# The second attention stream of the first half starts after the first one's end

## Chip, cores and metric

One core of a Trainium2 chip runs the whole program. The metric is the device time of one execution in microseconds, the median of several runs. TensorE is called PE, VectorE DVE, ScalarE ACT, GpSimd POOL and SyncE SP, as in the profile.

## What is computed

Two layers on 1024 tokens of width 1024, in fp32. Layer 0 mixes tokens by a recurrent scan (RWKV-7, eight heads) and a sliding-window attention (eight query heads, two key/value heads, window 128, with sinks) side by side; layer 1 by a convolution. Each layer then has an MLP with squared ReLU.

```python
def hybrid_mixer(h, w_in, ...):
    p = h @ w_in
    y_rwkv = rwkv7_time_mix(p[..., :o1], ...)
    y_att = sliding_window_sink_attention(q, k, v, sinks)
    return jnp.concatenate([y_rwkv, y_att], axis=-1) @ w_out

for layer in range(2):
    h = rmsnorm(x, norm_mix_g[layer])
    x = x + (hybrid_mixer(h, ...) if layer == 0 else conformer_conv(h, ...))
    x = x + sqrelu_mlp(rmsnorm(x, norm_ffn_g[layer]), w1, w2)
return rmsnorm(x, final_norm_g)
```

Attention takes, per block of 128 queries, the 256 keys of this and the last block, adds a slope by distance, takes the maximum with the sink, and divides the exponentials by their sum and the sink's.

## The kernel before

The tokens are worked in two halves of 512. Every large matrix product goes by `mm3` (L302 to L310): weights and inputs are split into a high part in fp32r and the rest, and three products of 128x512 are summed (L308, L309, L310). The weights come through SP's queue (L286), ACT rounds the high part (L291), and DVE or POOL takes the rest (`lo`, L272).

The first 800 us or so are woven. `weave` (L82) runs a base, the weight products of the two halves, the output projection of half 0 and its MLP, and beside it other generators: "A" and "B" run the scans (`scans`, L1100; B takes head pairs 0 and 2 of half 0, A takes 1 and 3 of half 0 and then all four of half 1), "n" the norm ahead of the MLP of half 0 (`norm0`, L505), and "0" and "1" the two streams of attention (`att`, L1024). A generator yields either a number, a time on the weave's own clock before which it isn't taken up again, or a flag that another sets. That clock is a planner's, advanced by written-down costs of PE work; the table LAG holds the pauses. Of the generators that are due the first in the order "1BAn0p" goes, as long as their share of PE work stays in bounds. The order so made is PE's order for good; the orders of the other engines and of the DMA queues are made by the scheduler of the language.

One stream of attention has two head pairs (stream 0 pairs 0 and 1, stream 1 pairs 2 and 3). For a pair it reads the queries back from DRAM into "raw" on SP's queue (`queries`, L1012; one buffer for both streams), rounds them on ACT (L1019) and takes the rest on DVE (L272), and makes two passes of 256 tokens (`attention`, L868): scores on PE (L890, L892) into PSUM tiles "at", of which there are two for both streams; slope and mask on DVE (L895), the maximum (L899), exponentials on ACT (L905), the division (L913 on ACT, L914 on DVE), transposes on PE (L923), copies on ACT (L924), the product with the values on PE (L932) and a copy on DVE (L936). The pause ATT stands between scores and transposes.

A scan of one head pair inverts 16x16 blocks on DVE (L705, L707), sends them through DRAM and back (L714 waits for that DMA), and joins them by four steps of block products on PE (L730), each with copies ahead of the next: L736 on ACT ahead of the second, L739 and L741 on DVE ahead of the third, L746 on ACT and L747 on DVE ahead of the fourth. The norm of half 0 sums squares on DVE (L455, L457, L477), transposes the sums on PE (L479), spreads the root by a product (L490, copied by ACT in L492), and scales on DVE (L517), with the split on ACT (L518) and DVE (L272). The residual sums of the output projection are L1192.

In half 0 stream 1 waits for the flag "0kv", set as soon as keys and values are in; in half 1 for "1z0", set when stream 0 has ended:

```python
        else:
            yield "1z0" if hf else "0kv"
```

Of the kernel before, what the change touches and what calls it, by code (L numbers as in the profile page):

```python
# [45 lines left out]
class Net:  # L46
# [977 lines left out]
    def att(self, hf, z):  # L1024

        if z == 0:
            for j in (18, 19):
                yield f"{hf}k{j}"
            if hf == 1:
                yield "mi1"  # L1030
                yield "att0"
            yield LAG["load"]
            yield from self.att_in(hf)
            self.done.add(f"{hf}kv")
        else:
            yield "1z0" if hf else "0kv"
        for i in (2 * z, 2 * z + 1):
            yield f"{hf}k{14 + i}"
            qs = self.queries(hf, i, z)
            yield LAG["query"]  # L1040
            yield from self.attention(hf, i, z, qs, self.mi[hf][4 + i])
        self.done.add(f"{hf}z{z}")
        self.natt += 1
        if self.natt == 2 * hf + 2:
            self.done.add(f"att{hf}")
# [400 lines left out]
    def run(self):  # L1446
# [75 lines left out]
        with self.tc.manual_schedule(engines={mybir.EngineType.PE}):  # L1522
            gs = {"p": params, "A": lambda: self.scans(0, [(0, 1), (0, 3), (1, 0), (1, 1), (1, 2), (1, 3)]), "B": scans_b,
                  "n": self.norm0, "0": lambda: att(0), "1": lambda: att(1)}
            self.weave(main(), *[gs[c]() for c in ORDER])
# [78 lines left out]
```

## Time and profile before

| | |
|---|---|
| median of 3 runs | 2353.58 us (2350.31 to 2355.61) |
| the profiled execution | 2348.04 us |
| its span, first to last instruction | 2346.3 us |
| PE busy | 2296.8 us (98%) |
| DVE busy | 1568.4 us (67%) |
| ACT busy | 1036.3 us (44%) |
| POOL busy | 349.1 us (15%) |
| mean granted clock of PE | 0.995 |

The span is the profiler's, from the first to the last instruction; the execution's own time has the launch around it. PE's idle time is the span less its busy time. A wait is read in the timeline, in square brackets behind the instruction that waited: how long its engine was idle, and what ended that.

### The profile page before, as it was taken

The page shows a single profiled execution, that of the slowest core. Times are in us where ns is not written, and L with a number is a line of the kernel's source. Part 1 is how long each engine was busy: PE and PEld are TensorE (multiplying, and loading weights), DVE is VectorE, ACT ScalarE, POOL GpSimd, SP SyncE. Part 2 cuts the span into 40 slices and gives each one's busy share as a digit, 9 for nine tenths or more (in the row PEclk, how much of TensorE's full clock was granted, in tenths as well). Part 3 has the DMA queues.
Part 4 walks back from the last instruction along what each step waited for, and adds up shares of the span by engine and source line. Part 5 has one row for each costly group of instructions (what it writes and reads, how often), then busy time and mean ns, then how long its engine had stood idle before and what let it go on. Part 6 is the DMA issues. An engine that isn't in the chain of part 4 may idle for free.

```text
span 2346.3 us, 38479 instructions
## 1 busy us (share of the span) xinstructions
PE 2296.8 (98%) x14535; PEld 1848.9 (79%) x14535; DVE 1568.4 (67%) x2707; ACT 1036.3 (44%) x1855; POOL 349.1 (15%) x333
## 2 busy tenths in 40 slices
PE   8989999999999999999999999999999999999998
PEld 6767777777777777878888888888878878888887
DVE  7876855767575655389876554789999746433334
ACT  6545625455353433353433464524433634433333
POOL 0001000000000000121000000215555422221221
PEclk9999999999999999999999999999999999999999
DMA  7445334445444454447666664563323333333332
GB/s 215 128 113 144 99 92 133 122 145 155 136 135 154 153 160 138 150 153 215 196 190 197 191 187 148 163 174 95 99 87 97 95 99 103 120 96 99 95 99 85
DMA packets 417933, 320.11 MB, mean 136 GB/s; under 512 B 44642, under 2 KB 360276, under 8 KB 417748
## 3 DMA queue, kind: packets, MB, share of 16 engines
q1 hardware_dynamic: 413684, 309.79, 44.0%
q0 software_dynamic: 2176, 4.19, 0.7%
q10 hardware_dynamic: 1888, 3.67, 0.5%
q8 instruction: 114, 1.87, 0.3%
q14 instruction: 71, 0.58, 0.1%
HBM read 257.29 MB, written 60.29 MB: 135 GB/s over the span
## 4 chain that ended last, share of the span: by engine, by line
PE 78%; DVE 15%; ACT 3%; issue 2%; DMA 2%; POOL 0%; SPq 0%; DVEq 0%; ACTq 0%; POOLq 0%
PE mm L308 23%; PE mm L309 22%; PE mm L310 22%; DVE acc L1318 8%; DVE hidl L272 1%; PE sc L648 1%; DVE x L1250 1%; PE sc L730 1%; PE sc L813 1%; PE at L932 1%; PE sc L767 1%; DVE wlo L272 1%; PE at L923 1%; PE sc L673 0%; DVE h L272 0%
## 5 line engine op out<-in xcount | busy, mean ns | idle before, releaser
L291 ACT CAST whi<-wraw 128x512 fp32r<-128x512 f32 x720 | 445.8, 620 | 979.6 <-PE mm L309 894.6
L308 PE MATMUL mm<-h,whi 128*128 128x512 f32 x1792 | 722.0, 404 | 7.4 <-DVE x L1250 3.0
L310 PE MATMUL mm<-h,wlo 128*128 128x512 f32 x1792 | 701.4, 392 | 1.0 <-POOL wlo L272 1.0
L309 PE MATMUL mm<-h,whi 128*128 128x512 f32 x1792 | 700.2, 391 | 1.3 <-DVE h L272 1.0
L1318 DVE SCALAR_TENSOR_TENSOR acc<-u,par,acc 128x512 f32<-128x512 f32 x480 | 429.3, 904 | 10.0
L272 DVE TENSOR_TENSOR wlo<-wraw,whi 128x512 fp32r<-128x512 f32 x370 | 260.7, 706 | 233.5 <-ACT whi L291 218.4
L308 PEld LDWEIGHTS mm<-h,whi 128*128 128x128 f32 x1792 | 337.2, 188 | 89.1 <-issue 12.5
L310 PEld LDWEIGHTS mm<-h,wlo 128*128 128x128 f32 x1792 | 337.4, 188 | 74.8 <-POOL wlo L272 1.9
L309 PEld LDWEIGHTS mm<-h,whi 128*128 128x128 f32 x1792 | 337.8, 188 | 68.7 <-issue 2.4
L308 PE MATMUL mm<-hidh,whi 128*128 128x512 f32 x992 | 389.7, 396 | 0.1
L309 PE MATMUL mm<-hidl,whi 128*128 128x512 f32 x992 | 386.2, 390 | 1.1 <-DVE hidl L272 0.9
L310 PE MATMUL mm<-hidh,wlo 128*128 128x512 f32 x992 | 384.5, 390 | 0.9 <-POOL wlo L272 0.9
L272 POOL TENSOR_TENSOR wlo<-wraw,whi 128x512 fp32r<-128x512 f32 x190 | 270.9, 1427 | 648.9 <-ACT whi L291 632.5
L1250 DVE TENSOR_TENSOR x<-mm,x 128x512 f32<-128x512 f32 x248 | 166.7, 687 | 85.0 <-PE mm L310 84.7
L308 PEld LDWEIGHTS mm<-hidh,whi 128*128 128x128 f32 x992 | 186.2, 188 | 43.0 <-issue 3.2
L309 PEld LDWEIGHTS mm<-hidl,whi 128*128 128x128 f32 x992 | 186.3, 188 | 40.7 <-DVE hidl L272 2.4
L310 PEld LDWEIGHTS mm<-hidh,wlo 128*128 128x128 f32 x992 | 186.2, 188 | 40.4 <-POOL wlo L272 1.3
L272 DVE TENSOR_TENSOR hidl<-rel,hidh 128x512 fp32r<-128x512 f32 x117 | 89.2, 763 | 78.1 <-ACT hidh L1227 76.7
L1223 ACT ACTIVATE rel<-rel 128x512 f32<-128x512 f32 x128 | 80.6, 633 | 4.6 <-DVE hidl L272 1.2
L1229 DVE CAST hidh<-rel 128x512 fp32r<-128x512 f32 x68 | 32.8, 485 | 71.2 <-ACT rel L1223 70.9
L1222 ACT ACTIVATE rel<-mm 128x512 f32<-128x512 f32 x128 | 75.6, 592 | 2.2 <-DVE hidl L272 2.0
L518 ACT CAST h<-nt 128x512 fp32r<-128x512 f32 x48 | 29.4, 622 | 34.7 <-DVE nt L517 34.3
(374 smaller groups left out, 2072.4 us busy)
## 6 DMA issues: line engine op xcount, KB each, us to landing
wraw<-in_mlp_w_dram SPq DMA_DIRECT2D x512, 256.0 KB
lo<-wlo SPq DMA_DIRECT2D x160, 256.0 KB
wlo<-lo SPq DMA_DIRECT2D x160, 256.0 KB
wraw<-in_cv_pw_w_dram SPq DMA_DIRECT2D x96, 256.0 KB
wraw<-in_hy_w_in_dram SPq DMA_DIRECT2D x80, 256.0 KB
wraw<-in_hy_w_out_dram SPq DMA_DIRECT2D x32, 256.0 KB
p<-stg SPq DMA_DIRECT2D x30, 256.0 KB
raw<-p SPq DMA_DIRECT2D x40, 128.0 KB
```

Source lines behind the costliest of these rows:

```text
L272: return eng.tensor_tensor(out=out, in0=x, in1=hi.bitcast(F32), op=ALU.subtract)
L291: nc.scalar.copy(out=hi, in_=raw)
L308: mm(ps, lhsT=whi, rhs=xhi, start=start, stop=False)
L309: mm(ps, lhsT=whi, rhs=xlo, start=False, stop=False)
L310: return mm(ps, lhsT=wlo, rhs=xhi, start=False, stop=stop)
L518: nc.scalar.copy(out=his[c], in_=t)
L648: mm(ps[64 * q:64 * q + 64, u * P:(u + 1) * P], lhsT=src[hs, c * 64:(c + 1) * 64], rhs=ar[hs, :, c, :], start=(u == 0), stop=(u == 3), ski ...
L1222: nc.scalar.activation(out=t, in_=ps, func=AF.Relu)
L1223: nc.scalar.activation(out=t, in_=t, func=AF.Square)
L1229: nc.vector.tensor_copy(out=hi, in_=t)
L1250: last = nc.vector.tensor_tensor(out=x, in0=pss[o], in1=x, op=ALU.add)
L1318: nc.vector.scalar_tensor_tensor(out=acc, in0=u[:, j:j + H], scalar=self.pv(f"dw{j}", c), in1=acc, op0=ALU.mult, op1=ALU.add)
```

## The change

One line of `att` changes. In half 0, too, stream 1 now waits for the flag that stream 0 sets when it has ended ("0z0"). In half 1 the text of the flag stays "1z0".

```diff
         else:
-            yield "1z0" if hf else "0kv"
+            yield f"{hf}z0"
         for i in (2 * z, 2 * z + 1):
             yield f"{hf}k{14 + i}"
             qs = self.queries(hf, i, z)
```

The weave fills PE anew from there on, and the scans come at other places too. Three places show it.

ACT, at the first block products of the first scan: L905 are exponentials of attention, L736 the copy behind the scan's first product, "asc" scores, "at" PSUM tiles. Before:

```order
L913 ACTIVATE asc<-asc,ams 128x256 x2
L291 CAST whi<-wraw 128x512 x2
L554 ACTIVATE sh<-stg,par 128x512
L905 ACTIVATE asc,ams<-asc,ams 128x256 x4
L908 ACTIVATE ams<-ams 128x4
L736 COPY BD<-sc_1628 128x256
L924 COPY asc<-at 128x512 x2
```

And now:

```order
L913 ACTIVATE asc<-asc,ams 128x256 x2
L291 CAST whi<-wraw 128x512 x2
L554 ACTIVATE sh<-stg,par 128x512
L291 CAST whi<-wraw 128x512
L736 COPY BD<-sc_1590 128x256
L924 COPY asc<-at 128x512 x2
```

The exponentials of stream 1 (L905, L908) no longer stand between.

DVE, at the norm of half 0: L1192 ends a column of the output projection, L714 and L716 take the inverted blocks of the first scan of half 1 from the DMA, L455 and L457 sum squares. Before:

```order
L1192 TENSOR_TENSOR x_4719<-mm,x_4719 128x512
L455 TENSOR_TENSOR acc<-sqt 128x512
L272 TENSOR_TENSOR wlo<-wraw,whi 128x512
L457 TENSOR_TENSOR acc<-acc,sqt 128x512 x2
L272 TENSOR_TENSOR wlo<-wraw,whi 128x512
L714 TENSOR_TENSOR C<-cx,bd_149 128x256
L716 TENSOR_TENSOR E<-cx,bd 128x512
L455 TENSOR_TENSOR acc<-sqt 128x512
L1192 TENSOR_TENSOR x_4719<-mm,x_4719 128x512
L457 TENSOR_TENSOR acc<-acc,sqt 128x512
```

And now:

```order
L1192 TENSOR_TENSOR x_4729<-mm,x_4729 128x512
L272 TENSOR_TENSOR wlo<-wraw,whi 128x512 x2
L714 TENSOR_TENSOR C<-cx,bd_149 128x256
L716 TENSOR_TENSOR E<-cx,bd 128x512
L1192 TENSOR_TENSOR x_4729<-mm,x_4729 128x512
L455 TENSOR_TENSOR acc<-sqt 128x512
L272 TENSOR_TENSOR wlo<-wraw,whi 128x512
L457 TENSOR_TENSOR acc<-acc,sqt 128x512 x2
L272 TENSOR_TENSOR wlo<-wraw,whi 128x512
L455 TENSOR_TENSOR acc<-sqt 128x512
L457 TENSOR_TENSOR acc<-acc,sqt 128x512
L1192 TENSOR_TENSOR x_4729<-mm,x_4729 128x512
```

L714 and L716 stand one column earlier, ahead of all the sums.

PE, at the start of the MLP of half 0: L730 are the block products of that same scan, the mm of L308 to L310 weight products, here the first of the MLP. Before, two weight products stood between the second step and the third, and as many between the others:

```order
L730 MATMUL sc_5583<-BD,E 32x32 x32
L730 MATMUL sc_5616<-E,BD 32x32 x32
L308 MATMUL mm<-h,whi 128x512
L309 MATMUL mm<-h,whi 128x512
L310 MATMUL mm<-h,wlo 128x512
L308 MATMUL mm<-h,whi 128x512
L309 MATMUL mm<-h,whi 128x512
L310 MATMUL mm<-h,wlo 128x512
L730 MATMUL sc_5658<-C,BD 32x32 x16
```

And now, where the weight product behind L1009 is the last of half 1's columns and the one at the end the first of the MLP:

```order
L730 MATMUL sc_5456<-C,BD 32x32 x32
L1009 MATMUL at<-ident,raw 128x128 x5
L308 MATMUL mm<-h,whi 128x512
L309 MATMUL mm<-h,whi 128x512
L310 MATMUL mm<-h,wlo 128x512
L730 MATMUL sc_5514<-BD,E 32x32 x32
L730 MATMUL sc_5547<-E,BD 32x32 x32
L730 MATMUL sc_5623<-C,BD 32x32 x16
L730 MATMUL sc_5642<-E,F 32x32 x16
L308 MATMUL mm<-h,whi 128x512
```

Steps two (two rows), three and four follow each other with nothing between.

## Rows read from the trace of the kernel before

**Rows 1.** Page, part 4: chain that ended last, share of the span by engine.

```profile
PE 78%; DVE 15%; ACT 3%; issue 2%; DMA 2%; POOL 0%; SPq 0%; DVEq 0%; ACTq 0%; POOLq 0%
```

**Rows 2.** Busy us of each engine, granted clock, DMA share, GB/s, by stretch.

```profile
100.00:400.00 300.00, 287.95 (x3383) 220.34 (x3376) 200.90 (x534) 147.31 (x298) 16.05 (x48) 0.98 0.41 116
400.00:800.00 400.00, 391.72 (x3427) 305.71 (x3426) 264.32 (x606) 193.01 (x371) 2.86 (x9) 1.00 0.46 140
```

**Rows 3.** PE timeline: start us, us, instruction, [us idle before <- releaser], 136 to 180.

```profile
136.19 0.75 PE L730 MATMUL sc<-C,BD 32*32 32x32 f32 x64
...
142.12 0.71 PE L730 MATMUL sc<-BD,E 32*32 32x32 f32 x62 [3.46 <-ACT BD L736]
...
151.76 1.29 PE L923 MATMUL at<-ident,asc 128*128 128x128 f32 x8 [1.46 <-DVE asc L895]
...
177.91 1.88 PE L923 MATMUL at<-ident,asc 128*128 128x128 f32 x8 [1.72 <-ACT asc L924]
```

**Rows 4.** ACT timeline, 139 to 142 us.

```profile
139.56 0.51 ACT L905 ACTIVATE asc<-asc,ams 128x256 f32<-128x256 f32 x1 [0.22 <-DVE ams L901]
...
141.63 0.35 ACT L736 COPY BD<-sc 128x256 f32<-128x256 f32 x1
```

**Rows 5.** Busy us and granted clock by stretch, where the clock fell.

```profile
140.00:155.00 15.00, 11.39 (x232) 9.04 (x233) 10.48 (x34) 6.84 (x23) 0.40 (x2) 0.77 0.36 90
175.00:185.00 10.00, 8.28 (x103) 6.22 (x97) 3.78 (x10) 4.11 (x8) 0.31 (x1) 0.83 0.26 76
```

**Rows 6.** PE timeline ahead of the first MLP, 455 to 473 us.

```profile
455.83 0.66 PE L479 MATMUL at<-ident,acc 128*128 128x128 f32 x4 [1.44 <-DVE acc L477]
...
458.54 1.12 PE L490 MATMUL at<-acc,ones 128*128 128x512 f32 x2 [0.66 <-DVE acc L485]
...
465.68 0.71 PE L1009 MATMUL at<-ident,raw 128*128 128x128 f32 x5
...
472.24 0.32 PE L730 MATMUL sc<-E,BD 32*32 32x32 f32 x13 [1.06 <-issue]
```

**Rows 7.** DVE timeline, same stretch.

```profile
451.01 0.43 DVE L714 TENSOR_TENSOR C<-cx,bd 128x256 f32<-128x256 f32 x1 [1.85 <-DMA cx<-d]
...
452.56 0.68 DVE L1192 TENSOR_TENSOR x<-mm,x 128x512 f32<-128x512 f32 x1
...
460.32 2.08 DVE L517 SCALAR_TENSOR_TENSOR nt<-x,par,acc 128x512 f32<-128x512 f32 x3 [1.24 <-ACT acc L492]
...
462.92 1.89 DVE L272 TENSOR_TENSOR h<-nt,h 128x512 fp32r<-128x512 f32 x3
...
473.38 0.41 DVE L739 TENSOR_TENSOR C<-sc,C 128x256 f32<-128x256 f32 x1
...
474.31 0.87 DVE L741 SCALAR_TENSOR_TENSOR E<-sc,rm,E 128x256 f32<-128x256 f32 x2
475.21 0.43 DVE L747 COPY F<-sc 32x256 f32<-32x256 f32 x1
```

**Rows 8.** ACT timeline, same stretch.

```profile
469.16 0.40 ACT L736 COPY BD<-sc 128x256 f32<-128x256 f32 x1
```

**Rows 9.** Busy us and granted clock by stretch, in a later stage.

```profile
1720.00:1730.00 10.00, 8.12 (x29) 6.25 (x28) 9.80 (x12) 1.24 (x2) 4.40 (x3) 0.83 0.18 52
```

**Rows 10.** PE timeline, second pair of scans, 240 to 265 us.

```profile
242.12 1.32 PE L923 MATMUL at<-ident,asc 128*128 128x128 f32 x8 [0.53 <-DVE asc L895]
...
246.57 1.09 PE L648 MATMUL sc<-ar,AG 64*64 64x128 f32 x16 [0.76 <-DVE ar L618]
...
263.47 1.15 PE L932 MATMUL at<-asc,vd 128*64 128x128 f32 x16 [1.09 <-ACT asc L924]
```

**Rows 11.** ACT timeline, a load of ACT tables.

```profile
482.62 0.59 ACT L774 COPY BD<-sc 128x512 f32<-128x512 f32 x1 [2.27 <-PE sc L767]
483.22 1.28 ACT L905 ACT_TABLE_LOAD   x1
484.52 0.51 ACT L905 ACTIVATE asc<-asc,ams 128x256 f32<-128x256 f32 x1
```

## The prediction

> **What bounds the kernel now.** I read the chain of waits first, because it says which engine the end hangs on: 78% of it is TensorE (PE) and 15% VectorE (DVE) [rows 1]. Then the busy time by stretch: from 100 to 400 us PE stands idle for 12.05 of 300 us and its mean granted clock is 0.98; from 400 to 800 us it is idle for 8.28 of 400 at full clock [rows 2]. So the end comes later by what PE waits and by what it loses to the clock, and the work of DVE, ScalarE (ACT), GpSimd and the DMAs costs only where PE stands for it. The program's order on PE is written by hand (the weave), so an instruction whose operand is late stops everything behind it.
>
> Then the timeline of PE where the two streams of half 0 run side by side. Three waits there are the streams' own [rows 3]. At 142.12 the second block product of a scan waits 3.46 us for the ACT copy L736. The first product began at 136.19 and takes 0.75, so its copy could have begun near 137; it runs at 141.63 because the four exponentials of the other attention stream (L905, the first at 139.56) stand ahead of it on ACT [rows 4]. At 151.76 the transposes of stream 1 wait 1.46 us for L895, the DVE reader of stream 0's scores: they come straight behind those scores, and both want one of the two PSUM tiles "at". At 177.91 transposes of one stream follow those of the other and wait 1.72 us for the copy L924.
>
> Then the granted clock of two stretches: its mean is 0.77 from 140 to 155 us, behind the first of these waits, and 0.83 from 175 to 185, at the third [rows 5]. Between the two levels, 1.2 and 2.4 GHz, that is 15 x 0.23 / 0.5 = 6.9 us and 10 x 0.17 / 0.5 = 3.4 us at the lower one.
>
> **The change part by part.** One wait moves: stream 1 of half 0 starts when stream 0 has ended, not when keys and values are in. Half 1 already waited so; there only the place beside the scan shifts. Nothing is added or removed on PE or DVE, so work alone would give 0. What moves is all of stream 1: two head pairs with two token halves each, 4 of the 8 passes of half 0, with their scores, exponentials, transposes and products, 8 DMA loads of "raw" on SP's queue, and two memsets on POOL. The places where an engine waits for them decide.
>
> (a) The three waits go: 3.46 + 1.46 + 1.72 = **6.64 us** [rows 3]. The order shows L736 without exponentials ahead of it. What could be late next there is the solve of the second scan on DVE, whose products PE now reaches sooner; it no longer shares DVE with stream 1's scores and splits, so I count nothing for it.
>
> (b) The slow clock goes with them. The wait at 151.76 lies in the 6.9 us, so the loss was (6.9 - 1.46) / 2 = 2.7; the second is 3.4 / 2 = 1.7: together **4.4 us** [rows 3, 5].
>
> (c) Before the first MLP, DVE waits 1.85 us for the DMA behind L714, ahead of the sums of the norm (L1192 at 452.56, 1.55 us after L714), and PE's transposes L479 wait 1.44 us for those sums [rows 6, 7]. The scan now starts one weight column earlier, L714 stands ahead of the sums with a column between, and the **1.44 us** go.
>
> (d) The same shift costs elsewhere. Before, pairs of weight products (two mm3, about 1.4 us) stood between the scan's products, and all of that waited 1.06 us in one place, at 472.24 [rows 6]. Now the column work ahead of the MLP runs out: products two, three and four stand back to back, before the MLP's first weight product. DVE is then scaling the norm: L517 takes 2.08 us for three, L272 1.89 for three [rows 7], and I count every other split (L272) like the latter, 0.63. From 460.32 on, seven L517 (4.9), six L272 of the norm (3.8) and two splits of weights (1.3) stand ahead of L739: 460.3 + 10.0, so it runs near 470, where before it stood at 473.38. PE has ended eight weight products and the first product (0.75 [rows 3]) by 465.7, where L1009 stood behind nine [rows 6], then L1009 and one more by 466.8; the copy L736 (0.40 [rows 8]) lets product two start after 0.2 and run to 468.3; product three comes at 470.4 (waits 2.1). Behind L739 (0.41) stand L517, a split, two L741 (0.87), a query's split, one L272, then L747 (0.43): 0.7 + 0.6 + 0.9 + 0.6 + 0.6 + 0.4 = 3.8, so product four comes at 474.2 (waits 3.2). 0.2 + 2.1 + 3.2 = 5.5 in place of 1.06: **+4.4 us**. Bounds: 0 if DVE runs ahead of this count by as much, and +8 if it falls behind by the 3.5 us that separate L739 here from L739 before.
>
> (e) Such a wait may bring the clock down. Nearest row: from 1720 to 1730 us PE was idle for 1.88 and the clock 0.83, that is 10 x 0.17 / 0.5 = 3.4 us low, a loss of 1.7 [rows 9]. I take **+1.7**, between 0 and half of the first dip, 3.4.
>
> (f) Stream 1 in its new place, beside the second pair of scans. There stream 0 and the scans already met 0.53, 0.76 and 1.09 us of waits [rows 10]; with one stream I expect as many as before, **0**, between -2.4 (all three gone) and +6.2 (one collision like that at 142, 3.46 + 2.7). The DMAs of "raw" and the memset are covered by PE's weight products; SP's loads of weights behind them are early.
>
> (g) The order holds 57 loads of ACT tables where 51 stood. One takes 1.28 us: the copy before it ends at 483.21, the load stands at 483.22 and the exponential at 484.52 [rows 11]. 6 x 1.28 = 7.7 us of ACT, which is busy for 147 of 300 us [rows 2]: I take **0**, with 7.7 as bound.
>
> The Trainium skill (ScalarE: Activation LUTs, section What ACT_TABLE_LOAD costs) speaks against this change here: it adds a drain to every switch and gives 2.66 us in all, which would make 16 us of ACT time. The trace does not agree: no gap of that size stands on either side of the load [rows 11].
>
> Sum: -6.64 - 4.4 - 1.44 + 4.4 + 1.7 = **-6.4 us**. The profiled execution took 2348.04 us (span 2346.3), so 2341.6; it lies 5.5 us under the median of the runs shown, 2353.58, against which I state the time: **2347.2 us**. A measurement of this kernel can tell about 0.2%, 4.7 us, from no change.
>
> **The rivals.** *The pause costs nothing* ((d) and (e) at 0): DVE is ahead and only the waits go: -6.64 - 4.4 - 1.44 = -12.5, 2341.1 us. For it: the norm's sums end 1.5 us earlier. Against it: the order of the three products, with no weight product between, is written down.
>
> *The gain is half given back.* The scans have tight places of their own (the waits in [rows 10]), and when one delay goes, PE reaches the next sooner; half of (a) and (b) comes back: -5.5 - 1.4 + 4.4 + 1.7 = -0.8, 2352.8 us, no change.
>
> *The table loads reach PE.* If each of the six delays a copy that PE waits for, +7.7: -6.4 + 7.7 = +1.3, 2354.9 us, no change. Against it: the copies that PE waits for stand mostly on DVE's side, and ACT is idle half the time [rows 2]. By the 2.66 us of that page of the Trainium skill it would be -6.4 + 16 = +9.6, 2363.2 us; the gapless rows speak against that.
>
> *Stream 1 collides with the second pair of scans* (slower). Its exponentials now queue on ACT beside the products of scans 2 and 3, where no attention stood; each time they pass an L736 or L746 that PE is about to want, it costs what 142.12 cost, 3.46 and 2.7 for the clock. One such place uses up the gain, two make -6.4 + 12.4 = +6.0, 2359.6 us: slower from two on. For it: one such collision is in the trace. Against it: it took the exponentials of one stream behind the scores of the other, which the change forbids, and its four passes are spread over some 100 us.
>
> That the change does nothing is excluded: the orders differ on PE from the place of the second stream's first scores on.
>
> **How the numbers follow.** The forecast 0.38, the free pause 0.12: faster by over 0.2%, 0.50. Half given back 0.33, tables 0.05: within 0.2%, 0.38. Two collisions 0.12: slower. The predicted time is the forecast's. The range reaches from the free pause, 2341.1, less 1.1 for a stall of (f) gone, to the no-change case, 2352.8, plus 2.7, half the spread of the runs shown (2350.31 to 2355.61): 2340.0 to 2355.5; it leaves out the collisions. The likeliest case's own range is 2345.5 to 2348.9, with (e) between none and its double.
>
> **What would show it.** Right: no wait of PE for L736 and no clock under 1.00 between 140 and 185 us; no wait at L479; waits of 2 and 3 us at the third and fourth L730 near 460 us, perhaps with a dip of the clock behind them. Wrong: (a) is wrong if PE's idle time from 100 to 400 us stays above 9 us; (d) is wrong if the L730 there wait under 2 us together; the slower rival is right if waits of 3 us stand at L730 or L923 between 260 and 380 us.

## Result and profile after

The change makes the kernel slower: 2374.84 us (median of three runs, 2374.11 to 2375.02) against 2353.58; ratio 1.0097, 95% interval 1.0082 to 1.0112. The forecast was 2347.2, with 2340.0 to 2355.5 as its range.

| profiled execution | before | after |
|---|---|---|
| its time, us | 2348.04 | 2374.11 |
| span, us | 2346.3 | 2372.4 |
| PE busy, us | 2296.8 | 2312.6 |
| PE idle, us | 49.5 | 59.8 |
| mean granted clock | 0.995 | 0.988 |
| ACT table loads | 51 | 57 |

PE executes the same 14535 matmuls in both. So the 26.1 us of span split into two parts: 10.3 us more of standing still, and 15.8 us more for the same work, which is the clock, as the sum below bears out. The medians lie 21.3 us apart; the profiled execution before took 5.5 us less than its median. The two stretches that answer to [rows 2], busy us of each engine, granted clock, DMA share and GB/s:

```profile
100.00:400.00 300.00, 283.99 (x3336) 216.31 (x3333) 196.27 (x526) 146.13 (x290) 16.26 (x48) 0.95 0.38 108
400.00:800.00 400.00, 386.07 (x3366) 301.69 (x3365) 254.51 (x590) 189.08 (x367) 2.72 (x8) 0.98 0.45 136
```

Idle time goes from 12.05 to 16.01 us in the first and from 8.28 to 13.93 in the second, together 9.6 of the 10.3. The loss is in half 0 and in half 1, where the line that changed does nothing but shift.

The same view of the six places between 100 and 800 us in which the clock fell, where before there were the two of [rows 5]:

```profile
145.00:155.00 10.00, 7.91 (x53) 6.45 (x54) 9.19 (x18) 2.69 (x5) 0.39 (x2) 0.66 0.26 80
235.00:250.00 15.00, 11.34 (x61) 8.76 (x60) 11.34 (x31) 9.08 (x20) 0.18 (x1) 0.66 0.09 26
290.00:300.00 10.00, 7.94 (x223) 6.30 (x212) 9.11 (x36) 4.80 (x10) 0.18 (x1) 0.83 0.34 108
310.00:325.00 15.00, 12.76 (x111) 9.80 (x112) 5.24 (x17) 6.05 (x17) 0.18 (x1) 0.66 0.21 64
480.00:495.00 15.00, 10.43 (x132) 8.24 (x121) 9.30 (x17) 5.41 (x11) 0.00 (x0) 0.77 0.50 155
555.00:565.00 10.00, 8.54 (x38) 6.68 (x38) 6.18 (x12) 4.05 (x8) 0.20 (x1) 0.66 0.38 118
```

By the prediction's arithmetic (length x what is missing to 1, over 0.5) that is 6.8 + 10.2 + 3.4 + 10.2 + 6.9 + 6.8 = 44.3 us at 1.2 GHz against 10.3 before; half of the 34 more is 17, near the 15.8.

Each of the six stands behind a wait. The PE timeline after (start, us, instruction, [us idle before <- releaser]):

```profile
147.09 0.58 PE L890 MATMUL at<-kh,q 128*128 128x256 f32 x1 [3.17 <-DVE mi L936]
...
239.89 1.12 PE L862 MATMUL sc<-ident,BD 128*128 128x128 f32 x4 [3.66 <-DVE BD L850]
...
292.41 0.66 PE L695 MATMUL sc<-ident,ar 128*128 128x128 f32 x4 [2.06 <-DVE krv L679]
...
313.36 0.34 PE L798 MATMUL sc<-vt,kt 64*64 64x64 f32 x4 [2.05 <-DVE ar L789]
...
481.83 0.25 PE L730 MATMUL sc<-C,BD 32*32 32x32 f32 x4 [1.67 <-DVE C L739]
483.02 0.63 PE L730 MATMUL sc<-C,BD 32*32 32x32 f32 x28 [0.94 <-issue]
484.93 0.31 PE L730 MATMUL sc<-E,F 32*32 32x32 f32 x2 [1.27 <-ACT F L746]
485.93 1.05 PE L730 MATMUL sc<-E,F 32*32 32x32 f32 x30 [0.69 <-DVE F L747]
...
546.44 0.66 PE L599 MATMUL sc<-ident,BD 128*128 128x128 f32 x4 [1.46 <-ACT BD L592]
...
556.46 2.13 PE L932 MATMUL at<-asc,vd 128*64 128x128 f32 x16 [2.95 <-ACT asc L924]
```

The three waits of [rows 3] and that at L479 [rows 6] are gone. The first two of the new ones fall where stream 0 is alone beside the scans, the next two where stream 1 now runs, the rest in half 1. What stood ahead of the releasing rows tells why. DVE at the first:

```profile
139.74 0.42 DVE L739 TENSOR_TENSOR C<-sc,C 128x256 f32<-128x256 f32 x1 [1.23 <-PE sc L730]
144.89 0.43 DVE L714 TENSOR_TENSOR C<-cx,bd 128x256 f32<-128x256 f32 x1 [4.73 <-DMA cx<-d]
...
146.62 0.41 DVE L936 COPY mi<-at 128x256 f32<-128x256 f32 x1
```

L936 empties the PSUM tile that the next scores (L890) want. The product that it copies had ended near 142, but in DVE's queue L936 stands behind L714, the inverted blocks of scan 1, which waits 4.73 us for their DMA. (The Trainium skill, PSUM — Partial Sum Buffer, section Engine vs sequencer instructions, says that the queues of ScalarE, VectorE and GpSimd are strictly first in, first out; these rows agree.) At 313 it is a DMA again, through two engines. ACT's copy of a query waits for the DMA, and DVE's split (L272) waits for ACT; the split stands ahead of the L788 and L789 that PE's L798 needs. ACT, then DVE:

```profile
311.22 0.62 ACT L1019 CAST q<-raw 128x512 fp32r<-128x512 f32 x1 [4.62 <-DMA raw<-p]
```

```profile
311.87 0.68 DVE L272 TENSOR_TENSOR q<-raw,q 64x512 fp32r<-64x512 f32 x1 [1.26 <-ACT q L1019]
...
312.81 0.40 DVE L789 TENSOR_TENSOR ar<-sc,ar 128x256 f32<-128x256 f32 x1
```

At 292 L679 stands behind the first step of an inversion, which waits for its blocks. At 240 no DMA is in it: DVE is busy without a gap, and L850 comes last behind an attention pass and the masks of another scan (L652). DVE, both places:

```profile
234.67 0.68 DVE L847 TENSOR_REDUCE m<-BD 128x8 f32<-128x512 f32 x1
235.26 1.21 DVE L899 TENSOR_REDUCE ams<-asc 128x4 f32<-128x1024 f32 x1
...
239.14 0.69 DVE L850 TENSOR_TENSOR BD<-BD,m 128x512 f32<-128x512 f32 x1
...
288.27 0.18 DVE L705 TENSOR_TENSOR C<-C,E 64x15 f32<-64x15 f32 x1 [2.40 <-DMA C<-d]
...
291.68 0.68 DVE L679 TENSOR_TENSOR krv<-sc,krv 128x512 f32<-128x512 f32 x1
```

And in half 1, on ACT, the copy L924 stands behind three table loads of a scan, as L592 at 545.67 stands behind two:

```profile
549.52 1.28 ACT L607 ACT_TABLE_LOAD   x1
...
551.97 1.28 ACT L603 ACT_TABLE_LOAD   x1
...
553.49 1.28 ACT L608 ACT_TABLE_LOAD   x1
...
555.83 0.58 ACT L924 COPY asc<-at 128x512 f32<-128x512 f32 x1
```

### The profile page after: what moved, and what is told of

Read it like the earlier page. It is cut to its first block, busy times and chain, and to the rows that moved or that the text cites. A ratio compares the mean times of both kernels' runs of the same rounds, so it can differ in the third digit from the quotient of the medians.

```text
span 2372.4 us, 38464 instructions
## 1 busy us (share of the span) xinstructions
PE 2312.6 (97%) x14535; PEld 1860.6 (78%) x14535; DVE 1569.8 (66%) x2707; ACT 1044.1 (44%) x1861; POOL 349.3 (15%) x333
## 3 DMA queue, kind: packets, MB, share of 16 engines
q10 hardware_dynamic: 1888, 3.67, 0.5%
q8 instruction: 114, 1.87, 0.4%
## 4 chain that ended last, share of the span: by engine, by line
PE 81%; DVE 11%; ACT 4%; DMA 2%; issue 2%; POOL 0%; SPq 0%; ACTq 0%; DVEq 0%; POOLq 0%
PE mm L308 24%; PE mm L309 23%; PE mm L310 23%; DVE acc L1318 5%; PE sc L730 1%; PE sc L648 1%; DMA raw<-p 1%; DVE hidl L272 1%; PE sc L813 1%; PE at L932 1%; DVE wlo L272 1%; PE sc L767 1%; ACT whi L291 1%; DVE h L272 0%; DVE x L1250 0%
## 5 line engine op out<-in xcount | busy, mean ns | idle before, releaser
L308 PE MATMUL mm<-h,whi 128*128 128x512 f32 x1792 | 727.1, 407 | 8.7 <-ACT h L383 3.1
L310 PE MATMUL mm<-h,wlo 128*128 128x512 f32 x1792 | 705.1, 394 | 1.4 <-POOL wlo L272 1.4
L272 DVE TENSOR_TENSOR wlo<-wraw,whi 128x512 fp32r<-128x512 f32 x370 | 261.0, 706 | 238.2 <-ACT whi L291 223.5
L308 PEld LDWEIGHTS mm<-h,whi 128*128 128x128 f32 x1792 | 339.7, 190 | 90.3 <-issue 10.7
L310 PEld LDWEIGHTS mm<-h,wlo 128*128 128x128 f32 x1792 | 339.9, 190 | 76.3 <-POOL wlo L272 2.3
L308 PE MATMUL mm<-hidh,whi 128*128 128x512 f32 x992 | 390.0, 396 | 0.1
L310 PE MATMUL mm<-hidh,wlo 128*128 128x512 f32 x992 | 384.9, 390 | 0.9 <-POOL wlo L272 0.9
L272 POOL TENSOR_TENSOR wlo<-wraw,whi 128x512 fp32r<-128x512 f32 x190 | 270.8, 1426 | 660.8 <-ACT whi L291 657.1
L308 PEld LDWEIGHTS mm<-hidh,whi 128*128 128x128 f32 x992 | 186.6, 188 | 43.5 <-issue 4.5
L310 PEld LDWEIGHTS mm<-hidh,wlo 128*128 128x128 f32 x992 | 186.6, 188 | 40.6 <-POOL wlo L272 1.3
L272 DVE TENSOR_TENSOR hidl<-rel,hidh 128x512 fp32r<-128x512 f32 x117 | 88.2, 755 | 79.5 <-ACT hidh L1227 78.1
L814 DVE TENSOR_TENSOR st<-sc,C 128x64 f32<-128x64 f32 x64 | 14.1, 220 | 48.4 <-PE sc L813 48.2
```

The source lines that it names most:

```text
L272: return eng.tensor_tensor(out=out, in0=x, in1=hi.bitcast(F32), op=ALU.subtract)
L308: mm(ps, lhsT=whi, rhs=xhi, start=start, stop=False)
L310: return mm(ps, lhsT=wlo, rhs=xhi, start=False, stop=stop)
```

## The experiments

Ratios are to the kernel before on the same chip, with 95% intervals. Single executions of one kernel differ by 10 us and more, so each kernel was timed in 6 to 12 of them. Where a term is under 5 us the rows are read instead of the median; they are of one execution each, and a single wait can differ between two executions of the same program, by 1.6 us under e4 and by 3.2 in the last section.

**e1 and e2: half 0 and half 1 apart.** One pause undoes the shift of half 1 in the kernel after (e1, shown), or makes it in the kernel before (e2, with a minus sign in place of the plus):

```diff
-        yield max(0.0, begun + LAG["ZD"] - self.clk)
+        yield max(0.0, begun + LAG["ZD"] + (5.75 if (hf, p) == (1, 0) else 0.0) - self.clk)
```

> The changed kernel, with the pause ahead of the first scan product of half 1's first scan 5.75 planner-us longer, which puts PE's order from there to the end back to that of the kernel before; half 0 keeps the two streams one behind the other. Theory L (every wait has its own local cause and price): in the stretch 400 to 800 the changed kernel had 13.9 us of PE idle against 8.3 before, and two stretches of 6.9 and 6.8 us at 1.2 GHz, half of which is lost. So 5.6 + 6.9 = 12.5 us come back: 2362 us, idle of 400 to 800 near 8.3, granted clock there 1.00, no wait at L730 near 480, at L599 near 546 or at L932 near 556; some 9 us of loss against the kernel before are left, all of it in 100 to 400. Theory S (the whole of the loss comes out of half 0, and half 1 only reads late): less than 3 us come back, 2372 or more.

> The mirror of it: the kernel before, both streams side by side in half 0, with that pause 5.75 planner-us shorter, so that only half 1 has the changed kernel's order. Theory L: the same 12.5 us are lost without any change in half 0: 2366 us, waits of about 1.7, 1.3 and 0.7 us at L730 near 460, and low clock behind them. Theory S: within 3 us of the kernel before, 2351 to 2357.

e1: 1.0054 (1.0037 to 1.0071), so 0.43% or 10.1 us come back; idle of 400 to 800 is 8.13 us, the clock there 1.00, and the waits at L599 and L932 are gone. e2: 1.0036 (1.0026 to 1.0046), 8.5 us lost with half 0's order untouched, and two of the rows of after, L599 with 1.46 and L932 with 2.95 us. At L730 it has other waits than after: 2.66 us for nothing that the profile shows, and 1.33 for L746. Half 1's order alone costs 8 to 10 us (12.5 were expected), half 0 some 13. Theory S falls.

**e3: the first wait's cause.**

```diff
-        tt(out=X.rearrange("p (g e c) -> p g e c", e=2, c=16), in0=cx[:, 0:8, :].unsqueeze(2).to_broadcast([P, 8, 2, 16]),
+        (gtt if (hf, p) == (0, 1) else tt)(out=X.rearrange("p (g e c) -> p g e c", e=2, c=16), in0=cx[:, 0:8, :].unsqueeze(2).to_broadcast([P, 8, 2, 16]),
```

and the same for L716; `gtt` is GpSimd's form of `tt`.

> The changed kernel, with the two products on the inverted blocks of scan 1 of half 0 (L714, L716) on GpSimd instead of VectorE: the same PE and ACT order, and VectorE's without these two rows. Theory L, VectorE's queue: the 4.73 us for which L714 waits for its DMA no longer stand ahead of the copy L936 that PE's L890 needs; the wait of 3.17 us at 147.09 goes, and with it most of the 6.8 us at 1.2 GHz between 145 and 155, of which half is loss: 2368 to 2371 us. Rival: the product L730 that follows at 148.25 is held by VectorE or GpSimd all the same and takes the wait over: 2373 to 2376.

1.0074 (1.0058 to 1.0090), some 5 us less than the change, with intervals that overlap a little. PE's and ACT's order is that of the change. The wait of 3.17 us is gone from the rows, and 16 us on there is another, which the change's profile did not have and e1's did (1.90):

```profile
162.89 0.34 PE L798 MATMUL sc<-vt,kt 64*64 64x64 f32 x4 [2.37 <-DVE ar L789]
```

The cause is the one named. That the second wait took over part of the gain is not shown. e1 has both waits, and ahead of this one ACT's copy of a query waits for its DMA, 2.98 us in e1, 2.35 here and 0.44 in the change's profile; so it seems to come and go with that landing.

**e4: meant to ask whether any shift is bad.** In the kernel before:

```diff
             yield "1z0" if hf else "0kv"
+            yield 0.0 if hf else 6.0
```

> The kernel before, with stream 1 of half 0 started 6 planner-us later and half 1's PE order word for word as it was: two streams side by side, only in another phase. Theory L: what counts is which row meets which; the wait of 3.46 us at 142 behind stream 1's exponentials moves or goes, others come: between 2347 and 2357, sign open. Rival T (any shift of a tuned order costs, whether or not the streams stand one behind the other): slower by 5 us or more, 2358.6 or above.

0.9997 (0.9984 to 1.0009), and it shows nothing of the question, for the edit moved nothing. Behind "0kv" stream 1 waits for the flag of its first query column ("0k16", in the loop below the pause), which is set only after the 6 planner-us are over. So the order on every engine is that of the kernel before, and rival T is left untested. It isn't excluded either: every kernel here with another order in half 0 has a ratio above 1, the nearest e11 with 1.0010 and e13 with 1.0015.

What e4 gives is a second profile of the kernel before. The waits of [rows 3], 3.46, 1.46 and 1.72 us, are 3.35, 3.09 and 1.89 in it.

**e5, e6, e7: repairs and other places for stream 1.** All three start from the kernel after and hold half 1 near its place before the change (e1's pause, here counted from a fixed time). e5 has e3's edit, GpSimd for the query splits (L272) of head pair 3, and the first line below. e6 has the middle lines, e7 the last one.

```diff
+        yield LAG["YD"] + (4.5 if (hf, p) == (0, 0) else 0.0)
...
+            yield "1z0" if hf else "0a0"
...
             yield from self.attention(hf, i, z, qs, self.mi[hf][4 + i])
+            self.done.add(f"{hf}a{i}")
...
             yield f"{hf}z0"
+            yield 0.0 if hf else 12.0
```

> The changed kernel with half 1's PE order put back as in e1, and three waits of half 0 taken at their causes: L714 and L716 of scan 1 on GpSimd (as in e3), the pause ahead of the last transposes of scan 0 4.5 planner-us longer (L862 comes when L850 is done), and the split of the queries of stream 1's second pair on GpSimd, so that VectorE does not stand behind their DMA. Theory L: against e1 (1.0054 of the kernel before) the wait of 3.20 us at 148 and some 1.5 us of low clock behind it go, the 3.67 us at 243 and half of the 8.6 us at 1.2 GHz behind it, and about 1 of the 1.84 us at 316 and 1 of clock: 14.5 us less, 2350 us, or up to 2357 if smaller waits follow. Rival M (a wait that is removed is taken over by the next product in the queue): 2360 or more.

> The changed kernel with half 1's PE order put back as in e1, but stream 1 of half 0 started when stream 0 has done its first pair of heads, 70 planner-us sooner than in the change and 64 later than before it. Theory P (the price of half 0 is the place beside the second pair of scans): the waits near 295 and 316 and the two stretches at 1.2 GHz behind them go, about 3.8 + 6 us; those near 148 and 243 stay: 2355. If overlap of the streams is what helps, in whatever place: 2351 to 2356 with the wait at 243 gone as well. If it is the scans alone that set the waits: as e1, 2362 to 2367.

> The changed kernel with half 1's PE order put back as in e1, and stream 1 of half 0 another 12 planner-us later: still alone and still beside the second pair of scans, in another phase. Theory L (single rows meet): the waits of 1.95 us at 295 and 1.84 us at 316 with their low clock, together some 10 us, move or go, and the time is anything between 2353 and 2368. Theory P: a stream of attention beside the second pair of scans costs its 10 us in any phase: 2362 to 2367, with new waits of 2 us or more between 270 and 360.

e5: 1.0060 (1.0042 to 1.0078), no better than e1; rival M. The pause went to the wrong scan: L862 at 243 belongs to scan 1, not 0. It moved the scans behind it all the same. Of the waits for another engine that came, the longest is again one behind a DMA, L747 behind scan 3's L714, which waits 2.72 us:

```profile
312.88 0.69 PE L730 MATMUL sc<-E,F 32*32 32x32 f32 x30 [3.77 <-DVE F L747]
```

e6: 1.0071 (1.0052 to 1.0089), though the waits at 295 and 316 are gone or smaller: the one at 148 grew to 5.22 us, and others of 1.17 to 1.98 came. e7: 1.0081 (1.0062 to 1.0099): those two went, and 2.62 us at L730 (303) and 2.51 at L862 (403) came. The first of these is the sign that theory P set for e7; the time of e7, 2372.85, is above P's range and theory L's. So e6 speaks against P, since a start half way between is no better, and e7 does not decide. The rows of all three show other pairs of rows meeting; none of these placings was good.

**e8, e11: the clock apart from the wait.** Useless products on PE ahead of L862:

```diff
+        for _ in range(8 if (hf, p) == (0, 1) else 0):
+            mm(ps[:, 0:256], lhsT=self.ones, rhs=self.rst[:, 0:256], start=True, stop=True)
```

> The kernel of e1 with eight products of 256 columns on constants put on PE right ahead of L862's transposes of scan 0, into the buffer that these then overwrite: 3.4 us of useless work in the wait of 3.67 us at 243. It separates the clock from the wait. Theory C (the clock falls because PE stood still): the end of the wait stays at 243, the 8.6 us at 1.2 GHz behind it go, and half of them is gained: 4.3 us less than e1, 2360 us, with no granted clock under 0.95 between 240 and 255. Rival: the clock falls with the scan's small products all the same: 2364 to 2367.

> What e8 meant to do, at the right scan: the kernel of e1 with eight products of 256 columns on constants (3.4 us of useless work, as e8's rows show) right ahead of L862's transposes of scan 1, where PE waits 3.67 us at 243. In e8 they stood at scan 0, where PE does not wait. Theory C (the clock falls because PE stood still): L862 still starts when L850 is done, and the 8.6 us at 1.2 GHz behind it go: granted clock 0.95 or more in 240 to 255, the matmuls of L308 to L310 behind it at 0.40 us and not 0.63, and 4.3 us less than e1: 2360. Rival: the clock falls all the same, 2364 to 2367.

e8 had them at scan 0 and shows nothing of the question (1.0052, 1.0035 to 1.0069). In e11 they fill the wait. PE's timeline of e1, from the last weight product ahead of the wait to the next transposes of a scan (L673):

```profile
239.07 0.39 PE L310 MATMUL mm<-h,wlo 128*128 128x512 f32 x1
243.13 1.11 PE L862 MATMUL sc<-ident,BD 128*128 128x128 f32 x4 [3.67 <-DVE BD L850]
243.90 0.78 PE L308 MATMUL mm<-h,whi 128*128 128x512 f32 x1
244.47 0.63 PE L309 MATMUL mm<-h,whi 128*128 128x512 f32 x1
...
252.02 0.60 PE L673 MATMUL sc<-ident,krv 128*128 128x128 f32 x4
```

And of e11, where two lines more shift L862 to L864:

```profile
234.99 0.40 PE L310 MATMUL mm<-h,wlo 128*128 128x512 f32 x1
235.23 3.62 PE L862 MATMUL sc<-rst,ones 128*128 128x256 f32 x16
239.02 0.66 PE L864 MATMUL sc<-ident,BD 128*128 128x128 f32 x4 [0.17 <-DVE BD L850]
239.43 0.48 PE L308 MATMUL mm<-h,whi 128*128 128x512 f32 x1
239.75 0.39 PE L309 MATMUL mm<-h,whi 128*128 128x512 f32 x1
...
244.00 0.60 PE L673 MATMUL sc<-ident,krv 128*128 128x128 f32 x4
```

The transposes start 4.0 us behind that product's start both times (243.13 - 239.07 and 239.02 - 234.99). From there to L673 it takes 8.89 us in e1, at 1.2 GHz, and 4.98 in e11. The rows between are the same in both. So 3.9 us of gain come from work of no use: the clock fell because PE stood still, theory C, with 4.3 expected. The whole kernel is at 1.0010 (0.9999 to 1.0020), 10 us under e1; the other 6 are not shown to be the fill's, for DVE's order changed a little with it and the wait at 164 is missing.

The price is not fixed. The same wait at L862, 3.63 to 3.67 us, is followed by some 3.3 us at 1.2 GHz in e8's profile, 6.9 in e10's and 10.2 in e1's.

**e9, e10: rows that wait for a DMA go to GpSimd**, all queries and inverted blocks of half 0, in the kernel before (e9) and in e1's (e10):

```diff
-            self.nc.scalar.copy(out=q, in_=t)
-            self.lo(q[lo, :], t[lo, :], q[lo, :], True)
+            (self.nc.gpsimd.tensor_copy if hf == 0 else self.nc.scalar.copy)(out=q, in_=t)
+            (self.nc.vector if hf else self.nc.gpsimd).tensor_tensor(out=q[lo, :], in0=t[lo, :],
+                in1=q[lo, :].bitcast(F32), op=ALU.subtract)
```

with L714 and L716 as in e3 for every scan of half 0. PE's order in the woven part stays in both: e9 has that of the kernel before, e10 that of e1. In the kernel before, the third wait of [rows 3], 1.72 us for the copy L924, had this row right ahead of that copy on ACT:

```profile
176.75 0.62 ACT L1019 CAST q<-raw 128x512 fp32r<-128x512 f32 x1 [3.73 <-DMA raw<-p]
177.27 1.07 ACT L924 COPY asc<-at 128x512 f32<-128x512 f32 x2
```

The second, 1.46 us for L895 at 151.76, is one of these too. On DVE L714 waits for its DMA ahead of it:

```profile
149.82 0.43 DVE L714 TENSOR_TENSOR C<-cx,bd 128x256 f32<-128x256 f32 x1 [1.93 <-DMA cx<-d]
...
150.86 1.41 DVE L895 SCALAR_TENSOR_TENSOR asc<-rel,at 128x256 f32<-128x256 f32 x4
```

> The kernel before (streams side by side), with the rows of half 0 that stand on ScalarE and VectorE behind a DMA put on GpSimd: the copies and splits of the queries (L1019, L272) and the products on the inverted blocks (L714, L716). PE's order in both halves' attention stays. Theory D (PE's waits come from ScalarE and VectorE rows queued behind a row that waits for a DMA): the waits of 1.46 us at 152 and 1.72 us at 178 go, with some 3 us of low clock's loss: 2346. Rival G (GpSimd takes the same waits in its own queue, and its copy ahead of the inversion, L700, comes late): 2352 or more.

> The same put on GpSimd in the kernel of e1 (half 0 one behind the other, half 1 as before the change). Theory D: the waits of 3.20 us at 148, 1.90 us at 164 and about 1 of the 1.84 us at 316 go, all three behind a DMA's landing on VectorE, and with them some 7 us of low clock's loss: 2351. The waits at 243 and 295 stay. Rival M (the next product takes the wait over): 2360 or more.

e9: **0.9980 (0.9967 to 0.9992)**, faster than both kernels, median 2349.04 against 2352.76; that lies between theory D's 2346 and rival G's 2352. Both waits are gone, and that at L736 (142) fell from 3.46 to 1.76, with the exponentials ahead of it some 3 us earlier. Idle of 100 to 400 falls from 12.05 to 6.89 us and the clock there is 1.00. GpSimd waits instead, and PE does not wait for it. Busy us by stretch of e9, and a row of its GpSimd:

```profile
100.00:400.00 300.00, 293.11 (x3431) 223.97 (x3426) 205.49 (x528) 151.36 (x300) 38.02 (x72) 1.00 0.42 119
```

```profile
162.86 0.61 POOL L1019 CAST q<-raw 128x512 fp32r<-128x512 f32 x1 [6.01 <-DMA raw<-p]
```

e10: 1.0017 (1.0003 to 1.0030), 8.7 us under e1 where 13.7 were expected. The waits at 148, 164 and 316 are gone, and so is that at 295, which was expected to stay; one of 1.33 at L786 came, and that at L862 (3.63) stays, as expected. With PE's order unchanged, moving these rows to another engine takes back 8.7 of the 12.7 us that e1 loses to the kernel before.

**e12, e13, e14: cover by pauses, and both repairs.** e12 has e3's edit and more planner time ahead of the steps that waited:

```diff
-        yield LAG["at"]
+        yield LAG["at"] + (2.4 if (hf, p) == (0, 2) else 0.0)
...
-            yield 0
+            yield 0 if q or (hf, p) not in ((0, 1), (0, 2)) else 2.6
...
-        yield LAG["YD"]
+        yield LAG["YD"] + (4.2 if (hf, p) == (0, 1) else 0.0)
```

e13 adds e10's GpSimd rows; e14 is e10 with the last of the three pauses alone.

> Half 0 one behind the other and half 1 as before, with each of e1's five waits of half 0 given cover by the planner: L714 and L716 of scan 1 on GpSimd, 4.2 planner-us more ahead of L862 of scan 1, 2.6 ahead of the first L798 of scans 1 and 2, 2.4 ahead of L695 of scan 2, so that PE has projections to do there. Theory L (local prices that add up): the waits of 3.20, 1.90, 3.67, 1.95 and 1.84 us go, 12.6 in all, and most of the 34 us at 1.2 GHz, half of which is loss: 2340 to 2345, faster than the kernel before. Rival M (each step that is moved meets another row): 2355 or more, with new waits of 2 us or more between 140 and 340.

> Half 0 one behind the other, half 1 as before, with the pauses of e12 and the queries and inverted blocks of e10 on GpSimd together. Theory Q (the loss of half 0 is queueing alone; the order one behind the other has no price of its own): against e12 (1.0017) the wait of 2.31 us at 159, where VectorE stands behind the split of the queries, goes with half of the 10 us at 1.2 GHz behind it; the wait of 3.06 at 297, behind the inversion's chain on VectorE, stays: 2349 us, the time of e9. Theory O (the order costs something by itself, because PE has only one stream's products for cover): 2355 or more.

> The kernel of e10 with one more edit: 4.2 planner-us more ahead of L862 of scan 1. Theory Q: of e10 (1.0017) the wait of 3.63 us at 237 and half of the 6 us at 1.2 GHz behind it go, 6 us: 2351. Rival M (the later scan meets another row): 2356 or more, with a new wait of 2 us or more between 230 and 340.

e12: 1.0017 (1.0005 to 1.0029), 8.7 us under e1, where theory L wanted it faster than the kernel before: four of five waits are covered, the one at L798 stays (2.31, behind a query's split), and 3.06 us at L730 (297) come anew, rival M's sign. e13: 1.0015 (0.9999 to 1.0030): no difference from the kernel before that can be told, but not e9's time either. Its one wait over 2 us is that at L730, 3.05 us for L747, which stands behind the inversion of scan 3 on DVE, with 6.9 us at 1.2 GHz behind it. e14: 1.0026 (1.0014 to 1.0038), no gain over e10: L862 no longer waits, and the same 3.05 us at L730 come in its place, rival M.

So most of half 0's loss was queueing behind rows that wait for a DMA, and could be taken back (e10). Whether the rest (e13 against e9, 0.35%) is that last wait or a price of streams one behind the other stays open; that wait was not taken away in a run.

## Why the prediction was wrong

The profile's view of the loss, us by the prediction's steps (half of the time at 1.2 GHz counted as loss):

| step | predicted | in the profile after |
|---|---|---|
| (a) three waits | -6.64 | -6.64; three gone |
| (a) "what could be late next", stream 0 alone | 0 | +3.17 +3.66, clock +8.5 |
| (b) low clock of the three waits | -4.4 | -5.2 |
| (c) L479 | -1.44 | -1.44 |
| (d) products back to back | +4.4 | +3.5 (4.57 in place of 1.06) |
| (e) clock behind it | +1.7 | +3.4 |
| (f) stream 1's new place | 0 (-2.4 to +6.2) | +2.06 +2.05 +0.5, clock +6.8 |
| (g) table loads | 0, bound 7.7 | +1.46 +2.95, clock +3.4 |

It sums to +28, against 26.1 of span. Waits that the table leaves out come to 5.2 us before and 4.6 after between 100 and 400 us; the three of [rows 10], 2.4 us, went among them. The table sets two single executions against each other: its half 1, (d), (e) and (g), comes to 14.7, where e1 and e2 show 8 to 10.

**(a)** names the step that failed: "What could be late next there is the solve of the second scan on DVE ... so I count nothing for it." It was late next: PE reached the next scores sooner, and L936 stood behind L714, which waited for the solve's blocks to come back by DMA (147). At 240 a step of the same scan that the prediction did not name, L850, stood behind an attention pass. The two took 15.3 us with the clock, where the sum had 0. e3 and e10 show the first cause. e11 shows the price of the second, and e12 and e14 that a later L862 does not wait. The row was there to be read: the wait at 151.76, which the prediction put down to the two tiles "at", already stood behind an L714 that waited 1.93 us for its DMA. The test that the prediction set was right: idle from 100 to 400 stayed above 9 us (16.01).

**(f)** was the other large miss, 11.4 us, or 9.0 with the waits of [rows 10] that went, against a bound of 6.2. The slower rival had the place (260 to 380 us) and not the row. It looked for ACT's exponentials ahead of L736 and L746; what came was DVE behind the DMAs of a query and of another scan's blocks, at L695 and L798. The bound failed because one collision of the kind at 142 was taken as the worst. Two came, and each brought its low clock. That the DMAs of "raw" are "covered by PE's weight products" is untrue of ACT and DVE, which wait for their landing in order (4.62 us on ACT at 311).

**(d)** holds in its waits: third and fourth product wait 1.67 and 1.96 us for DVE and ACT (2.1 and 3.2 predicted). The 1.06 that it took off is misread: that wait is for no copy, and neither is the 0.94 after; both belong to the stall of the last section. **(e)** lies at its upper end.

**(c)** holds in its size and its row, but it is not "the same shift" as (d). e1, which undoes (d), keeps L714 a column earlier on DVE and has no wait at L479. e2, which makes (d), has L714 in its old place and this row:

```profile
456.26 0.66 PE L479 MATMUL at<-ident,acc 128*128 128x128 f32 x4 [1.92 <-DVE acc L477]
```

So (c) comes with half 0's order and (d) with half 1's.

**(b)** was right for its own stretches, and a little low: from 150 to 155 us the granted clock is 0.93, so the wait at 151.76 lies for the most part behind the slow stretch and need not be taken off. The term belongs to every new wait as well. In e11's pair a wait of 3.67 us went with 3.9 us of clock, 7.6 together.

**(g)**: table loads did stand ahead of copies that PE waited for, in half 1, where the order of L905, L592 and L924 changed by one pause. e1 and e2 show that half 1's order has a price, and these rows put part of it on ACT. But of the six new loads only one is in half 1's order (L608 at 553.49; e1 has 56 loads and e2 52); the others at this place stand in the kernel before too and met an attention pass only now. No run took the loads alone away, so their share is argued, and that 1.46 + 2.95 + 3.4 lies near the bound of six loads, 7.7, is chance. Each load is 1.28 us in the rows. The 2.66 us of the Trainium skill (ScalarE: Activation LUTs, section What ACT_TABLE_LOAD costs) was not needed.

Of the rivals, "the gain is half given back" had the right mechanism for half 0 (PE reaches the next tight place sooner) and far too small a price: more came back than had gone.

## What to carry to other kernels

Before taking a wait away, look at what PE meets next, and read the queue of the engine that releases it: a row that waits for a DMA delays everything queued behind it, ready or not. Put such rows on an engine that nobody waits for (here GpSimd, 15% busy), as e9 does; that was worth 0.2% with PE's order as it was, while moving a stream to another time (the change, e6, e7) exchanged one set of collisions for another. And price a wait of PE like these for the clock behind it too, as a range: 7.6 us for 3.67 in e11's pair, an estimated 2.06 + 1.7 for the one at 292 and 2.05 + 5.1 for the one at 313. An edit to a planned order should first be seen to change the order: e4's did not.

## What was not expected of the hardware

PE stood still in the midst of 64 small products of one step, waiting for nothing that the profile shows, and then ran at 1.2 GHz. First in e10, then in e4, which has the program of the kernel before:

```profile
469.07 0.65 PE L730 MATMUL sc<-E,BD 32*32 32x32 f32 x53
474.04 0.36 PE L730 MATMUL sc<-E,BD 32*32 32x32 f32 x9 [4.31 <-issue]
474.33 0.80 PE L308 MATMUL mm<-h,whi 128*128 128x512 f32 x1
```

```profile
471.64 0.62 PE L730 MATMUL sc<-E,BD 32*32 32x32 f32 x49
476.52 0.43 PE L730 MATMUL sc<-E,BD 32*32 32x32 f32 x13 [4.26 <-issue]
```

At this place the profiles of the kernels with half 1's old order, or near it, have 0.3 us (e8, e13), 0.8 to 1.1 (e12, e1, before, e11), 2.4 (e7) and 3.5 to 4.6 (e14, e9, e5, e4, e10, e6). A transfer of the queue named "instruction", 0.02 MB, falls between the two rows of e10 (471.7 to 472.7). The lengths follow it: in all sixteen profiles PE goes on 1.2 to 1.5 us behind the landing of such a transfer near this step, whether it lands early or late. In the kernel before it lands at 470.8 and PE goes on at 472.2, in e4 at 475.1 and 476.5, in e10 at 472.7 and 474.0. The Trainium skill (Runtime: NRT & Kernel Launch, section Instruction fetch mechanics) says that instructions come in blocks of 16 KiB and that crossing a block's end is mostly hidden; the 114 transfers with 1.87 MB in the page of the change agree with the size, and the 4 us do not agree with "hidden". No run moved the transfer, so the cause is read from rows alone, and why it lands late is open. With the clock behind it, the stall is as large as most terms here. Between the two profiles of the kernel before it is 4.26 us for 1.06, and 10.4 us at 1.2 GHz for none from 470 to 490: an estimated 8 us, where the spans differ by 6.5 (2352.8 and 2346.3). So it is a large part of why these two executions of one program differ, and it weighs on every comparison of rows above.
